# An encoder block with product-key experts on one core: lo parts on GpSimd, one more dense product ahead of the gate build, loads on another queue

## The chip, the cores and the metric

The program runs on one core of one Trainium2 chip. The metric is the time of one execution on the device in microseconds (us); lower is better. TensorE (PE) multiplies matrices, VectorE (DVE) and ScalarE (ACT) work element by element, GpSimd (POOL) does the gathers and a few small operations, and SyncE (SP), ScalarE and GpSimd issue DMAs.

## What is computed

One layer: adaLN modulation, an attention group and a gated MLP group side by side, an output projection, and then the PEER sub-layer, which takes most of the time. For each of 512 tokens and 8 heads it scores 2 x 128 keys, takes the best 16 of each half, the best 16 of the sums, and adds up 128 of 16384 one-neuron experts:

```python
def peer(h, w_q, keys, U, V):
    q = (ht @ w_q).reshape(T, PEER_HEADS, 2, PEER_HALF_DIM)
    s1 = jnp.einsum('thd,hkd->thk', q[:, :, 0], keys[:, 0])
    s2 = jnp.einsum('thd,hkd->thk', q[:, :, 1], keys[:, 1])
    v1, i1 = lax.top_k(s1, PEER_TOPK)
    v2, i2 = lax.top_k(s2, PEER_TOPK)
    cand = (v1[..., :, None] + v2[..., None, :]).reshape(T, PEER_HEADS, PEER_TOPK * PEER_TOPK)
    sc, ci = lax.top_k(cand, PEER_TOPK)
    idx = i1[ci // PEER_TOPK] * PEER_N_KEYS + i2[ci % PEER_TOPK]
    gates = jax.nn.softmax(sc, axis=-1)
    ...
        a = jnp.einsum('chkd,cd->chk', U[ids], xb)
        w = jax.nn.gelu(a, approximate=False) * g
        return jnp.einsum('chk,chkd->cd', w, V[ids])
```

All of it is float32. A float32 product is made of three TensorE products of a hi part (a rounded copy, made by ScalarE) and a lo part (what the rounding left, made by a subtraction): hi by hi, hi by lo, lo by hi (`mm3`, lines 84 to 88; `split_into`, lines 80 to 82).

## The kernel before

The experts are done in two ways. For the first 352 tokens they are dense: the 16384 experts are 128 tiles of 128, `a = gelu(U h2)` for every token and expert of tile e (a dense product, `a_mm`, 8 parts of 3 matmuls, tile `pa`), multiplied by a gate matrix that is zero for the experts not chosen, and then `w V` (tiles `out`). For the last 160 tokens, which are a block of 128 (the gathered block, names with g) and 32 more (names with x), the chosen rows of U and V are gathered by GpSimd and VectorE adds them up.

The stages of the second half, in order:

1. The score stage (the loop over `h` at line 729). `score(h)` makes two query products `q` (24 matmuls each, weights `wq`), copies them (`qT`), multiplies them with the keys (`sc`) and copies the scores to `s_sb` (dense tokens) and `s_gb`; the latter goes out to DRAM as `sgd`. Behind it `dense` products of the expert tiles from 2 on are placed, one for each head, and LATE = 8 more at the last head. Their operand comes from `a_load(e)`: a load of `u_t[e]`, and `split_into`, so a hi part (`u8h`) by ScalarE and a lo part (`u8l`) by VectorE; hi and lo have two buffers each, the loads three. Then VectorE takes the best 16 of each score row (`route_keys`, 5 operations each); after the fourth and the eighth head it does the candidates, picks and lookups of four heads, which end in `i1a` and `i2a`.
2. The gate build (lines 775 to 865), 44 steps for 8 tokens each: one-hot tiles `o` by VectorE and ScalarE, `gg` by TensorE, copies by ScalarE. Its order on TensorE, ScalarE and VectorE is written out by hand, and the dense products that are left up to tile 29 (`nu = AHEAD - ahead` of them) are laid in between, their loads and lo parts with them.
3. The expert loop (line 1051), 128 turns: a dense product 30 tiles ahead, the cast and lo part of V, the gates, and `out`. Between its turns a list of small jobs (`fill`) does the routing of the gathered block and its gathers. `gb_open` and `gb_scores` read that block's scores back from `sgd`, two heads in buffers (`sgb`).

Outside the hand-written parts the order of each engine's instructions is laid out when the program is built, by priorities in the order of the program and assumed costs. At run time each engine takes its own instructions in that order, and an instruction that waits for a semaphore holds those behind it on its engine, DMA issues included.

Of the kernel before, what the change touches and what calls it, by code (L numbers as in the profile page):

```python
# [25 lines left out]
PH = 8  # L26
# [9 lines left out]
NE = 128  # L36
AHEAD = 30
FIRST = 2
LATE = 8
TAIL = 4  # L40
END = 3
HG = 4
# [19 lines left out]
def tile_kernel(ctx: ExitStack, tc: tile.TileContext, a: dict, out: bass.AP):  # L62
    nc = tc.nc
# [16 lines left out]
    def split_into(hi, lo, src, eng=None):  # L80
        nc.scalar.copy(hi, src)
        last_lo[0] = (eng or nc.vector).tensor_sub(lo, src, hi.bitcast(F32))
# [27 lines left out]
    sgd = tc.dram_tile([P, 2 * PH, P], F32, name="sgd")  # L110
# [13 lines left out]
    with ExitStack() as fr:  # L124
# [141 lines left out]
        with ExitStack() as s1st:  # L266
# [43 lines left out]
            for kh in range(2):  # L310
                hi, lo = wl[kh]
# [158 lines left out]
        qkv_st.close()  # L470
        up = pool(ctx, "upool", side="right")

        def a_load(e):
            raw = up.tile([P, KD, P], F32, name=f"u{e}r", tag="ur", bufs=3)
            nc.sync.dma_start(raw, a["u_t"][e])
            hi = up.tile([P, KD, P], F32R, name=f"u{e}h", tag="uh", bufs=2)
            lo = up.tile([P, KD, P], F32R, name=f"u{e}l", tag="ul", bufs=2)
            split_into(hi, lo, raw)
            return hi, lo

        X = pool(right, "X2", side="right")
# [35 lines left out]
    def a_mm(e, p, hl, c):  # L517
        mm3(p[:, :TD], (hl[0][:, c, :], hl[1][:, c, :]), (h2T[0][:, c, :TD], h2T[1][:, c, :TD]),
            c == 0, c == KD - 1)

    def a_psum(e):
        return psa.tile([P, 512], F32, name=f"pa{e}", tag="pa", bufs=2)

    def a_gelu(e, p):
        t = ar.tile([P, TD], F32, name=f"a{e}", tag="a", bufs=AHEAD + 1)
        nc.scalar.activation(t, p[:, :TD], AF.Gelu)  # L526
        a_tiles[e] = t
# [17 lines left out]
    def route_tiles(pl, tag, nb, nh):  # L545
        r = {"nb": nb, "nh": nh, "pl": pl, "tag": tag}
        r["v12"] = pl.tile([P, nb, nh, 2, K], F32, name=f"v12{tag}", tag="v12", bufs=1)
        r["i12"] = pl.tile([P, nb, nh, 2, K], U32, name=f"i12{tag}", tag="i12", bufs=1)
        return r

    def route_keys(r, b, h, f, sv):
        tmp = r["pl"].tile([P, P], F32, name=f"tmp{r['tag']}{b}{h}{f}", tag="tmp", bufs=2)
        top16(r["v12"][:, b, h, f, :], r["i12"][:, b, h, f, :], sv, tmp)

    def route_cands(r):
        n = r["nb"] * r["nh"]
        v = r["v12"].rearrange("p b h f k -> p (b h) f k")
        cand = r["pl"].tile([P, n, NC], F32, name=f"cd{r['tag']}", tag="cand", bufs=1)
        for r0, nr, ncol, p0 in STAIR:
            sh = [P, n, nr, ncol]  # L560
            nc.vector.tensor_tensor(
                cand[:, :, p0:p0 + nr * ncol].rearrange("p b (i j) -> p b i j", j=ncol),
                v[:, :, 0, r0:r0 + nr].unsqueeze(3).to_broadcast(sh),
                v[:, :, 1, :ncol].unsqueeze(2).to_broadcast(sh), op=ALU.add)
        r["cand"] = cand
        r["ci"] = r["pl"].tile([P, n, K], U32, name=f"ci{r['tag']}", tag="ci", bufs=1)

    def route_pick(r, b, h, sc):
        i = b * r["nh"] + h
        cand2 = r["pl"].tile([P, NC], F32, name=f"ce{r['tag']}{i}", tag="cand2", bufs=2)  # L570
        top16(sc, r["ci"][:, i, :], r["cand"][:, i, :], cand2)

    def route_decode(r):
        pl, tag, ci = r["pl"], r["tag"], r["ci"]
        n = r["nb"] * r["nh"]
        rt_ = lambda m, dt=F32: pl.tile([P, n, K], dt, name=f"{m}{tag}", tag=m, bufs=1)
        t3, t2 = rt_("t3", U32), rt_("t2", U32)
        nc.vector.tensor_single_scalar(t3, ci, 3, op=ALU.logical_shift_right)
        nc.vector.tensor_single_scalar(t2, ci, 2, op=ALU.logical_shift_right)
        row, st, u = rt_("row"), rt_("rst"), rt_("ru")  # L580
        rcf = pl.tile([P, 2, n, K], BF16, name=f"rcf{tag}", tag="rcf", bufs=1)
        nc.vector.scalar_tensor_tensor(row, t3, 5.0, t2, op0=ALU.add, op1=ALU.max)
        nc.vector.scalar_tensor_tensor(row, row, 42.0, ci, op0=ALU.add, op1=ALU.max)
        nc.vector.tensor_scalar(row, row, -48.0, 0.0, op0=ALU.add, op1=ALU.max)
        nc.vector.tensor_copy(rcf[:, 0], row)
        nc.vector.tensor_scalar(st, row, 7.0, 8.0, op0=ALU.mult, op1=ALU.add)
        nc.vector.tensor_scalar(u, row, 3.0, 24.0, op0=ALU.mult, op1=ALU.add)
        nc.vector.scalar_tensor_tensor(st, row, 15.0, st, op0=ALU.mult, op1=ALU.min)
        nc.vector.scalar_tensor_tensor(st, u, 48.0, st, op0=ALU.min, op1=ALU.min)
        nc.vector.tensor_add(st, st, row)  # L590
        nc.vector.tensor_sub(rcf[:, 1], ci, st)
        r["rcf"] = rcf

    def route_tables(r):

        pl, tag = r["pl"], r["tag"]
        n = r["nb"] * r["nh"]
        i12f = pl.tile([P, n, 2, K], BF16, name=f"i12f{tag}", tag="i12f", bufs=1)
        nc.scalar.copy(i12f, r["i12"].rearrange("p b h f k -> p (b h) f k"))
        r["i12f"] = i12f  # L600
        r["rep"] = {}

    def route_rep(r, f):
        n = r["nb"] * r["nh"]
        t = r["pl"].tile([P, n, K, K], BF16, name=f"rep{r['tag']}{f}", tag="rep", bufs=1)
        nc.scalar.copy(t, r["i12f"][:, :, f, :].unsqueeze(3).to_broadcast([P, n, K, K]))
        r["rep"][f] = t
# [29 lines left out]
    with ExitStack() as qs:  # L637
# [45 lines left out]
        RD = pool(rd, "rdense", side="right")  # L683
        R = pool(qs, "route")
        keys = R.tile([P, 2 * PH, P], F32, name="keys_s")
        nc.gpsimd.dma_start(keys, a["keysT"])
        wq = {}

        def load_wq(i):
# [11 lines left out]
        def score(h):  # L701
            s_sb = R.tile([P, ND, 2, P], F32, name=f"s{h}", tag="s_sb", bufs=3)
            s_gb = R.tile([P, 2, P], F32, name=f"sg{h}", tag="s_gb", bufs=2)
            for f in range(2):
                i = 2 * h + f
                p = q_ps(f"q{i}")
                hi, lo = wq.pop(i)
                for j in range(KD):
                    mm3(p, (hi[:, j, :], lo[:, j, :]), (h2T[0][:, j, :], h2T[1][:, j, :]),
                        j == 0, j == KD - 1)  # L710
                if i + 2 < 2 * PH:
                    load_wq(i + 2)
                qT = W.tile([P, T], F32, name=f"qT{i}", tag="qT", bufs=3)
                nc.scalar.copy(qT, p)
                p = q_ps(f"sc{i}")
                for b in range(NB):
                    nc.tensor.matmul(p[:, b * P:(b + 1) * P], lhsT=qT[:, b * P:(b + 1) * P],
                                     rhs=keys[:, i, :], start=True, stop=True)
                nc.scalar.copy(s_sb[:, :, f, :], p[:, :TR].rearrange("p (b n) -> p b n", n=P))
                nc.scalar.copy(s_gb[:, f, :], p[:, TR:])  # L720
            nc.sync.dma_start(sgd[:, 2 * h:2 * h + 2, :], s_gb)
            scores[h] = s_sb

        i1a, i2a, sca, gts = [RD.tile([P, ND, PH, K], F32, name=n) for n in ("i1a", "i2a", "sca", "gts")]
        ahead = FIRST
        score(0)
        r = None
        nxt = a_load(ahead)
        for h in range(PH):
            if h + 1 < PH:  # L730
                score(h + 1)
            while ahead < FIRST + h + 1 + (LATE if h == PH - 1 else 0):
                hl, nxt = nxt, None
                p = a_psum(ahead)
                for c in range(KD):
                    a_mm(ahead, p, hl, c)
                nxt = a_load(ahead + 1)
                a_gelu(ahead, p)
                ahead += 1
            s_sb = scores.pop(h)  # L740
            hl = h % HG
            if hl == 0:
                r = route_tiles(R, f"d{h}", ND, HG)
            for b in range(ND):
                for f in range(2):
                    route_keys(r, b, hl, f, s_sb[:, b, f, :])
            if hl == HG - 1:
                hs = slice(h - HG + 1, h + 1)
                route_tables(r)
                route_rep(r, 0)  # L750
                route_cands(r)
                for b in range(ND):
                    for i in range(HG):
                        route_pick(r, b, i, sca[:, b, h - HG + 1 + i, :])
                route_decode(r)
                route_lookup(r, 0, i1a[:, :, hs, :])
                route_rep(r, 1)
                route_lookup(r, 1, i2a[:, :, hs, :])
# [16 lines left out]
    with ExitStack() as gs:  # L775
# [63 lines left out]
        for k in range(nu):  # L839
            e = ahead + k  # L840
            s0 = k * NG // nu
            st = {}
# [11 lines left out]
        ahead = AHEAD  # L854
# [18 lines left out]
    st = {}  # L873
# [9 lines left out]

    def gb_scores(h):
        st["sg"][h] = st["R"].tile([P, 2, P], F32, name=f"sgb{h}", tag="sg", bufs=2)
        nc.sync.dma_start(st["sg"][h], sgd[:, 2 * h:2 * h + 2, :])

    def gb_keys(h, f):
        if f == 0 and h + 1 < PH:
# [277 lines left out]
```

## Time and profile before

| what | value |
|---|---|
| median of 3 runs | 1520.97 us (1518.54 to 1521.08) |
| the profiled execution | 1520.59 us, of which the span of its instructions is 1518.8 us |
| TensorE busy | 1439.7 us (95%) |
| VectorE busy | 1287.3 us (85%) |
| ScalarE busy | 634.6 us (42%) |
| GpSimd busy | 489.4 us (32%) |
| DMA | 410.94 MB, mean 271 GB/s |

The busy time of TensorE counts matmuls from start to modelled end, so a full busy time is not yet TensorE at its peak. In the timelines each row is an instruction or several equal ones: start, length, engine, line, operation, what it writes and reads, shapes, and in brackets the idle time of that engine just before it and what ended it. The granted clock is the share of TensorE's full clock that it was given.

### The profile page before, as it was taken

How to read it: one execution, taken by the hardware profiler on the slowest of the kernel's cores; microseconds unless marked ns; L12 is line 12 of the kernel's file. 1: busy time of each engine (PE TensorE's matmuls, PEld its weight loads, DVE VectorE, ACT ScalarE, POOL GpSimd, SP SyncE). 2: the span in 40 equal slices, each digit the busy share in tenths (PEclk: the TensorE clock that was granted, in tenths of full speed). 3: DMA queues.
4: the chain of work that ended last, by engine and by line, in shares of the span. 5: the costliest groups of instructions: out<-in, count | busy, mean ns of one | idle time of the engine just before them, and what ended most of it. 6: DMA issues, size and time to landing. Idle time of an engine off the chain costs nothing.

```text
span 1518.8 us, 21628 instructions
## 1 busy us (share of the span) xinstructions
PE 1439.7 (95%) x7623; PEld 1235.6 (81%) x7623; DVE 1287.3 (85%) x2476; ACT 634.6 (42%) x1078; POOL 489.4 (32%) x400
## 2 busy tenths in 40 slices
PE   2899899999888999999999999999999999999997
PEld 1666677888788999888888888888888888888774
DVE  6947865569899997899999999998999999998776
ACT  2533433535257897333433333333333333333333
POOL 1212100000000000222354676666665555544420
PEclk9999999999998999999999999999999999999999
DMA  9626443332143779899799999999999999997863
GB/s 367 233 98 206 141 153 125 132 105 67 52 164 105 227 220 267 309 327 307 268 402 400 372 376 380 379 361 378 369 387 373 380 366 378 379 357 274 306 216 117
DMA packets 154332, 410.94 MB, mean 271 GB/s; under 512 B 13008, under 2 KB 58720, under 8 KB 154096
## 3 DMA queue, kind: packets, MB, share of 16 engines
q1 hardware_dynamic: 100720, 216.49, 40.1%
q0 software_dynamic: 51568, 187.17, 33.8%
q10 hardware_dynamic: 1936, 5.90, 1.1%
q8 instruction: 60, 0.98, 0.3%
q14 instruction: 48, 0.39, 0.1%
HBM read 381.24 MB, written 28.28 MB: 270 GB/s over the span
## 4 chain that ended last, share of the span: by engine, by line
PE 73%; DVE 13%; DMA 6%; ACT 4%; issue 3%; POOL 0%; SPq 0%; POOLq 0%; DVEq 0%; ACTq 0%
PE out L86 10%; PE out L88 10%; PE out L87 10%; PE pa L88 9%; PE pa L87 9%; PE pa L86 9%; DMA wada<-w_ada 2%; PE gg L822 2%; PE q L87 1%; PE q L88 1%; PE q L86 1%; ACT o L816 1%; PE yo L87 1%; PE yo L88 1%; PE yo L86 1%
## 5 line engine op out<-in xcount | busy, mean ns | idle before, releaser
L908 POOL DMA_INDIRECT gug<-peer_u,idx x128 | 200.3, 1565 | 104.6 <-DVE scrg L931 72.0
L908 POOL DMA_INDIRECT gvg<-peer_v,idx x128 | 162.0, 1266 | 159.6 <-DVE accg L945 141.0
L908 POOL DMA_INDIRECT gux<-peer_u,idxx x32 | 43.4, 1356 | 449.8 <-DMA u34r<-u_t 342.9
L945 DVE SCALAR_TENSOR_TENSOR accg<-gvg,wgg,accg 128x1024 f32<-128x1024 f32 x127 | 163.8, 1290 | 1.3
L931 DVE SCALAR_TENSOR_TENSOR scrg<-gug,h2gg 128x1024 bf16<-128x1024 f32 x128 | 156.2, 1221 | 1.3
L822 PE MATMUL gg<-o,o 128*128 128x128 f32 x704 | 88.4, 280 | 2.7 <-ACT o L816 1.6
L822 PEld LDWEIGHTS gg<-o,o 128*128 128x128 f32 x704 | 86.0, 196 | 4.7 <-ACT o L816 4.7
L1074 DVE TENSOR_TENSOR a<-a,g 128x352 f32<-128x352 f32 x128 | 64.9, 517 | 5.7 <-DMA g<-gd 3.4
L816 ACT ACTIVATE o<-o1b,gT 128x128 f32<-128x128 bf16 x176 | 58.2, 406 | 13.4 <-PE gg L822 6.8
L155 DVE SCALAR_TENSOR_TENSOR macc<-wada,csil,macc 128x1024 f32<-128x1024 f32 x40 | 51.3, 1282 | 10.8 <-DMA wada<-w_ada 10.5
L526 ACT ACTIVATE a<-pa 128x352 f32<-128x352 f32 x128 | 58.3, 456 | 1.5 <-PE pa L88 1.4
L805 DVE TENSOR_TENSOR o<-iota_s,gT 128x1024 f32<-128x1024 f32 x44 | 53.8, 1223 | 1.0 <-PE gg L822 0.9
L908 POOL DMA_INDIRECT gvx<-peer_v,idxx x32 | 40.2, 1256 | 33.4 <-DVE accx L945 23.6
L809 DVE TENSOR_SCALAR o<-iota_s,gT 128x128 f32<-128x128 f32 x176 | 49.1, 347 | 0.0
L831 ACT COPY st<-gg 128x512 f32<-128x512 f32 x88 | 46.3, 581 | 0.0
L931 DVE SCALAR_TENSOR_TENSOR scrx<-gux,h2gx 128x1024 bf16<-128x1024 f32 x32 | 39.0, 1218 | 3.3 <-DMA gux<-peer_u,idxx 3.3
L945 DVE SCALAR_TENSOR_TENSOR accx<-gvx,wgx,accx 128x1024 f32<-128x1024 f32 x31 | 40.0, 1291 | 0.3
L141 POOL DMA_DIRECT2D wada<-w_ada x32 | 17.2, 537 | 60.4 <-DVE macc L155 24.4
L165 PE MATMUL mcol<-ident_s,macc 128*128 128x128 f32 x32 | 7.4, 389 | 27.4 <-DVE macc L152 23.2
L165 PEld LDWEIGHTS mcol<-ident_s,macc 128*128 128x128 f32 x32 | 5.5, 200 | 29.0 <-DVE macc L152 18.1
L430 ACT ACTIVATE pe<-s,mx 128x512 f32<-128x512 f32 x16 | 11.0, 690 | 28.9 <-DVE mx L428 21.6
L120 POOL TENSOR_TENSOR n_r<-n_ms,nhalf 128x1 f32<-128x1 f32 (+1 forms) x5 | 3.6, 717 | 54.7 <-DVE n_ms L118 54.7
(2817 smaller groups left out, 4971.7 us busy)
## 6 DMA issues: line engine op xcount, KB each, us to landing
gd<-st SPq DMA_DIRECT2D x11, 1984.0 KB
g<-gd SPq DMA_DIRECT2D x31, 704.0 KB
wada<-w_ada POOLq DMA_DIRECT2D x32, 512.0 KB
wada<-w_ada SPq DMA_DIRECT2D x16, 512.0 KB
x<-x SPq DMA_DIRECT2D x4, 512.0 KB
x<-x ACTq DMA_DIRECT2D x4, 512.0 KB
x2d<-x ACTq DMA_DIRECT2D x4, 512.0 KB
gug<-peer_u,idx POOLq DMA_INDIRECT x128
```

Source lines behind the costliest of these rows:

```text
L86: nc.tensor.matmul(o, lhsT=lh, rhs=rh, start=first, stop=False)
L87: nc.tensor.matmul(o, lhsT=lh, rhs=rl, start=False, stop=False)
L88: nc.tensor.matmul(o, lhsT=ll, rhs=rh, start=False, stop=last)
L155: nc.vector.scalar_tensor_tensor(acc, w, csil[:, c:c + 1], acc, op0=ALU.mult, op1=ALU.add)
L526: nc.scalar.activation(t, p[:, :TD], AF.Gelu)
L805: nc.vector.tensor_tensor(o2s[n], iota.unsqueeze(1).to_broadcast([P, UT, P]), tT[:, 1, t0:t0 + UT].unsqueeze(2).to_broadcast([P, UT, P]), ...
L816: nc.scalar.activation(o1s[n][:, i, :], e[:, :, i], AF.Copy, scale=tT[:, 2, t0 + i:t0 + i + 1])
L822: nc.tensor.matmul(pgs[n][i // 4][:, i % 4 * P:(i % 4 + 1) * P], lhsT=o2[:, i, :], rhs=o1[:, i, :], start=True, stop=True)
L908: nc.gpsimd.indirect_dma_start(out=g, out_offset=None, in_=src, in_offset=bass.IndirectOffsetOnAxis(ap=ix[:, s:s + 1], axis=0))
L931: nc.vector.scalar_tensor_tensor(scr, g, 1.0, gs_[k]["h2g"], op0=ALU.mult, op1=ALU.mult, accum_out=actg[:, n:n + 1])
L945: nc.vector.scalar_tensor_tensor(accg, g, wg[:, s:s + 1], accg, op0=ALU.mult, op1=ALU.add)
L1074: nc.vector.tensor_tensor(wv3, wv3, gt[:, :, e % GE, :], op=ALU.mult)
```

## The change

Three things. `a_load` takes an engine for the subtraction, and the score loop passes GpSimd for tiles 2 to 9, placed on GpSimd's queue behind the load of the keys. LATE goes from 8 to 9, so that tile 18's dense product stands in the score loop and the gate build has 11 in place of 12. And the loads of the gathered block's scores go on ScalarE's queue in place of SyncE's.

```diff
-LATE = 8
+LATE = 9
...
-        def a_load(e):
+        def a_load(e, eng=None):
             raw = up.tile([P, KD, P], F32, name=f"u{e}r", tag="ur", bufs=3)
             nc.sync.dma_start(raw, a["u_t"][e])
             hi = up.tile([P, KD, P], F32R, name=f"u{e}h", tag="uh", bufs=2)
             lo = up.tile([P, KD, P], F32R, name=f"u{e}l", tag="ul", bufs=2)
-            split_into(hi, lo, raw)
+            with ExitStack() as order:
+                if eng is not None:
+                    order.enter_context(tc.issue_after(keyed.ins))
+                split_into(hi, lo, raw, eng)
             return hi, lo
...
-        nc.gpsimd.dma_start(keys, a["keysT"])
+        keyed = nc.gpsimd.dma_start(keys, a["keysT"])
...
-        nxt = a_load(ahead)
+        nxt = a_load(ahead, nc.gpsimd)
...
-                nxt = a_load(ahead + 1)
+                nxt = a_load(ahead + 1, nc.gpsimd if ahead + 1 < FIRST + PH else None)
...
-        nc.sync.dma_start(st["sg"][h], sgd[:, 2 * h:2 * h + 2, :])
+        nc.scalar.dma_start(st["sg"][h], sgd[:, 2 * h:2 * h + 2, :])
```

## Rows read from the trace of the kernel before

**Rows 1.** Windows: stretch, length; PE, PEld, DVE, ACT, POOL busy; PEclk, DMA share, GB/s.

```profile
290.00:350.00 60.00, 60.00 (x302) 50.32 (x301) 39.03 (x192) 17.77 (x32) 0.00 (x0) 1.00 0.31 96
350.00:400.00 50.00, 45.76 (x222) 38.36 (x221) 48.90 (x238) 21.26 (x31) 0.00 (x0) 0.93 0.18 59
400.00:460.00 60.00, 50.99 (x293) 47.02 (x292) 53.39 (x231) 26.77 (x34) 0.00 (x0) 0.95 0.36 119
620.00:700.00 80.00, 75.82 (x393) 65.84 (x392) 76.37 (x216) 29.50 (x43) 24.10 (x17) 1.00 0.91 328
800.00:900.00 100.00, 100.00 (x526) 88.40 (x526) 91.81 (x118) 35.67 (x50) 60.90 (x42) 1.00 1.00 383
```

**Rows 2.** Timeline of TensorE, score stage: q12, u8l's wait, q15.

```profile
376.99 0.48 PE L86 MATMUL q<-h2T,wq12h 128*128 128x512 f32 x1
...
387.06 0.66 PE L88 MATMUL pa<-h2T,u8l 128*128 128x352 f32 x1 [3.93 <-DVE u8l L82]
...
406.24 0.48 PE L86 MATMUL q<-h2T,wq15h 128*128 128x512 f32 x1
```

**Rows 3.** Timeline of ScalarE, score stage: casts of u8, wq11, wq12.

```profile
355.42 1.08 ACT L81 CAST u8h<-u8r 128x1024 fp32r<-128x1024 f32 x1
358.18 1.05 ACT L81 CAST wq11h<-wq11r 128x1024 fp32r<-128x1024 f32 x1 [1.68 <-PE q L87]
...
366.31 1.05 ACT L81 CAST wq12h<-wq12r 128x1024 fp32r<-128x1024 f32 x1 [4.70 <-PE q L87]
```

**Rows 4.** Timeline of VectorE, score stage: u8l, and its longest idle time.

```profile
385.78 1.23 DVE L82 TENSOR_TENSOR u8l<-u8r,u8h 128x1024 fp32r<-128x1024 f32 x1
...
414.21 1.22 DVE L82 TENSOR_TENSOR u10l<-u10r,u10h 128x1024 fp32r<-128x1024 f32 x1 [5.00 <-ACT u10h L81]
```

**Rows 5.** Timeline of VectorE and TensorE, start of the score stage: u2.

```profile
270.46 1.22 DVE L82 TENSOR_TENSOR u2l<-u2r,u2h 128x1024 fp32r<-128x1024 f32 x1
...
272.69 0.32 PE L88 MATMUL pa<-h2T,u2l 128*128 128x352 f32 x1
...
272.85 0.33 PE L86 MATMUL pa<-h2T,u2h 128*128 128x352 f32 x1
```

**Rows 6.** GpSimd's groups by shape: count | busy us, mean ns | idle us.

```profile
L120 POOL TENSOR_TENSOR rq_r<-rq_ms,nhalf 128x4 f32<-128x4 f32 x1 | 1.0, 1037 | 5.8 <-DVE rq_ms L118 5.8
...
L100 POOL MEMSET ones<- 128x128 f32 x1 | 0.2, 229 | 0.0
...
L102 POOL MEMSET nhalf<- 128x8 f32 x1 | 0.1, 129 | 0.0
```

**Rows 7.** Timeline of TensorE ahead of the gate build.

```profile
458.93 0.47 PE L782 MATMUL gt<-ident_s,i2a 128*128 128x128 f32 x1 [5.82 <-DVE i2a L623]
```

**Rows 8.** Timeline of VectorE in the gate build: one operation of three steps.

```profile
501.04 1.22 DVE L805 TENSOR_TENSOR o<-iota_s,gT 128x1024 f32<-128x1024 f32 x1
...
505.38 1.22 DVE L805 TENSOR_TENSOR o<-iota_s,gT 128x1024 f32<-128x1024 f32 x1
...
507.87 1.22 DVE L805 TENSOR_TENSOR o<-iota_s,gT 128x1024 f32<-128x1024 f32 x1
```

**Rows 9.** Timeline of SyncE's DMA issues, start of the expert loop.

```profile
594.88 4.30 SPq L475 DMA_DIRECT2D u34r<-u_t  x1
...
599.74 0.90 SPq L886 DMA_DIRECT2D sgb<-sgd  x2
...
617.76 0.32 SPq L886 DMA_DIRECT2D sgb<-sgd  x1
```

**Rows 10.** Timeline of VectorE, start of the expert loop.

```profile
605.97 0.49 DVE L539 MAX8 v12g<-sgb 128x8 f32<-128x128 f32 x2 [3.49 <-DMA sgb<-sgd]
...
615.49 0.29 DVE L539 MAX8 v12g<-sgb 128x8 f32<-128x128 f32 x1 [3.88 <-DMA sgb<-sgd]
```

**Rows 11.** Timeline of ScalarE, start of the expert loop.

```profile
622.67 1.05 ACT L1070 CAST v4h<-v4r 128x1024 fp32r<-128x1024 f32 x1 [9.44 <-DMA v4r<-peer_v]
```

**Rows 12.** Timeline of TensorE, start of the expert loop.

```profile
622.10 0.50 PE L88 MATMUL out<-v3h,w3l 128*128 128x512 f32 x1 [1.72 <-DVE w3l L82]
```

## The prediction

> **What bounds the kernel now.** I read the page first, then the windows by stage, then the timelines of the places where TensorE stands idle. On the page TensorE is the busiest engine by far, so a change pays where it takes idle time or a slow clock from TensorE. The windows show where that is [rows 1]. From 800 us on TensorE is busy 100.00 of 100 us, and from 290 to 350 us 60.00 of 60. Idle time lies between 350 and 460 us (4.24 and 9.01 us, at a granted clock of 0.93 and 0.95) and between 620 and 700 us (4.18 us). The loop behind 700 us is full of TensorE's work, so what is won ahead of it should come out at the end almost whole.
>
> **The score stage.** Between the scores TensorE works in a fixed order: a query product `q`, some matmuls of a dense product `pa`, the score matmuls `sc`. From the start of q12 to that of q15, three such steps, it takes 406.24 - 376.99 = 29.25 us [rows 2]. A regular step is 8.13 us: ScalarE casts the query weights once a step, wq11h at 358.18 and wq12h at 366.31 us [rows 3]. In the first of the three steps the order has `pa` matmuls on u8's lo part ahead of the scores, and TensorE stands 3.93 us for it [rows 2]. The hi part had been there since 355.42 + 1.08 = 356.50 us [rows 3]; the lo part ran on VectorE only at 385.78 us [rows 4], behind the routing of the first four heads. The slow clock of this window comes with that stall.
>
> **Removing that wait.** With u2 to u9 on GpSimd, u8l can be made right behind u8h, some 25 us before it is wanted. Three regular steps are 24.39 us, so the last scores come 29.25 - 24.39 = **4.9 us** earlier. What is late next? VectorE, which must be done with the earlier heads by then. Ahead of the last scores it idles 5.00 us [rows 4], and it loses two lo parts of 1.23 us (u8, u9); so at least 5.00 + 2.46 - 4.9 = 2.6 us of idle time are left, and the scores still end last. The other six lo parts (u2 to u7) fall where VectorE is busy 39.03 of 60 us and TensorE all 60 [rows 1]: they win nothing. From 414 us on VectorE is the chain, until i2a, the last index that the gate build waits for; all of this moves up by 4.9 us. Bounds: 0, if another wait takes the place of u8l's; 7.7 us, if all that TensorE loses from 350 to 400 us comes back (4.24 us idle and 0.07 of 50 us by the clock [rows 1]).
>
> **What a lo part costs on GpSimd.** The trace has no such subtraction on that engine. On VectorE it takes 1.22 us [rows 5], the lower bound. On GpSimd a memset of 128 columns takes 0.229 us and one of 8 columns 0.129 us [rows 6], so 0.0008 us a column and 0.9 us for 1024; two reads and a write at that rate give 2.7 us, which I take. The far end is a `pow` row, 1.037 us for 4 columns [rows 6], which would be over 260 us for 1024. I hold that for the price of `pow` and give it 1 in 100. A dense product lasts about two steps, 16 us, in this stage, and two lo buffers stand ready, so anything under 16 us hides behind the queries. The exception is u2, the first: its lo part began at 270.46 and TensorE used it at 272.69 us [rows 5]; at 2.7 us it is ready at 273.1, **0.4 us** late (0 to 1.5). GpSimd's queue has nothing else in this stage; the load of the keys is kept ahead of the lo parts by the order that the change adds.
>
> A rule speaks against the move. The Trainium skill, "GPSIMD Engine Reference", 3.1, has a two-input add take 1.96 times as long as on VectorE, and the Trainium skill, "SBUF — State Buffer", Who interferes with whom, says that a VectorE instruction with two SBUF inputs and a GpSimd instruction that reads SBUF shut each other out for their whole length. By these, as an estimate, a lo part takes 2.4 us and can hold VectorE as long; no run here shows it yet. For u8 and u9 that would be 4.8 us where 2.6 us are left, and the sum would be 2.2 us worse.
>
> **Nine dense products.** One `pa` product (u18) moves from the gate build to the stretch ahead of it, and with it u19's load, cast and lo part. TensorE's 24 matmuls, 3.84 us at 0.16 us from start to start [rows 5], fit into the 5.82 us for which it waits for i2a [rows 7]. VectorE, which sets that end, gets one lo part more: +1.2 us. In the gate build a VectorE step takes 507.87 - 505.38 = 2.49 us, and one with a lo part in it 505.38 - 501.04 = 4.34 us [rows 8]; one less there is worth 1.85 us. Net **-0.6 us**. Bounds: +1.2 us, if nothing comes back in the build; -2.6 us, if TensorE is its true limit and the whole 3.84 us come back.
>
> **Scores on ScalarE's queue.** The loads of the gathered block's scores, `sgb`, stand in SyncE's order behind loads that wait. The first goes out at 599.74 us, behind u34r's issue of 4.30 us [rows 9]; VectorE stands 3.49 us for it until 605.97, and 3.88 us for the third until 615.49 us [rows 10]. SyncE in its turn stands until 617.76 us at the fifth [rows 9], and v4r behind it goes out only then; ScalarE idles 9.44 us for v4r [rows 11]. TensorE loses 1.72 us waiting for w3l [rows 12], which VectorE makes behind all this. On ScalarE the first load need not wait for u34r and can go some 5 us earlier, and v4r no longer stands behind the fifth. I take the wait for w3l as gone, **-1.7 us**. The eight issues cost ScalarE 0.32 to 0.45 us each, as on SyncE [rows 9], in a stretch where it is busy 29.50 of 80 us [rows 1]. From the third on a load waits until VectorE has read the scores two loads before, and behind it on ScalarE stand the casts of u, v and w. Bounds: -4.2 us, all of TensorE's idle time from 620 to 700 us, and +2 us, if casts are held.
>
> **The sum.** -4.9 + 0.4 - 0.6 - 1.7 = -6.8 us. The profiled execution took 1520.59 us, 1.8 of it outside the span, and lies 0.4 us under the median of 1520.97. 1520.6 - 6.8 = **1513.8 us**.
>
> **The rivals.**
> *The wait moves.* The order of every engine is laid out anew at the build, from assumed costs. The 3.93 us come from one misjudged place, and another may arise: VectorE held in the routing of the first four heads, or TensorE placed ahead of a lo part on GpSimd. For it: VectorE is busy 48.90 of 50 us there [rows 1]. Against it: the 25 us of lead. Then 1.3 of the 4.9 us are left and half of the queue's share: -1.3 + 0.4 - 0.6 - 0.9 = -2.4, 1518.2 us, up to 1520.
> *More comes out.* Half-way from the sum to all the good bounds (-7.7 - 2.6 - 4.2 = -14.5): -10.7, 1509.9 us.
> *ScalarE is held (slower).* A load of `sgb` that stands ahead of casts holds them until VectorE has caught up. One hold of 9.44 us [rows 11] came with 1.72 us lost on TensorE [rows 12]. Six loads wait for a buffer; if each is laid so far ahead of its release, that is 6 x 1.7 = 10 us in place of the 1.7 won: 1520.6 - 5.1 + 10 = 1525.5 us. It decides from holds over about 9 us. Against it: the casts have gaps there, and every load wants a buffer that VectorE frees in its own order.
> *Nothing.* If the last scores don't set the end of the routing, the small terms are left, 1519 us.
>
> **How the numbers follow.** Forecast (its own range 1511 to 1517) 0.57; the wait moves 0.16; more comes out 0.11; ScalarE held 0.13; nothing 0.03. About 0.2%, 3.0 us, is what a measurement of this kernel can tell from no change. Faster by more, under 1517.9: forecast and more comes out, 0.68. Slower, over 1524.0: 0.13. Within: 0.19. The range goes from 1508 to 1522 us: it takes in the moved wait and the bounds that are not at their ends together, and leaves out most of the slower case.
>
> **What would show it.** Right: u8l and u9l on GpSimd soon behind their casts, 2 to 3 us each; no TensorE wait over 1 us among the queries; q12 to q15 in some 24.4 us; i2a 3.7 us earlier (TensorE goes on at 455 in place of 458.93); the first `sgb` at VectorE by 601 us; no 1.7 us wait for w3l. Wrong: VectorE's two-input operations longer beside GpSimd; a new wait among the queries; ScalarE idle with a load of `sgb` at its head while TensorE waits for a cast; a gain that is there by 460 us and gone by 700.

## The result and the profile after

| what | before | after |
|---|---|---|
| median | 1521.03 us (1518.54 to 1521.65) | 1510.43 us (1509.14 to 1511.65) |
| ratio, 95% interval | | 0.9937 [0.9922, 0.9953] |
| profiled execution (span) | 1520.59 us (1518.8) | 1509.24 us (1507.5) |

The kernel is faster by 0.6%; the forecast of 1513.8 us is 3.4 us above the median, and its sign and range hold. The two profiled executions differ by 11.3 us, where the working had 6.8. The windows by stage, which answer to [rows 1], show TensorE's idle time from 350 to 400 and from 620 to 700 us gone, and 3.75 of 9.01 us of that between 400 and 460 us (columns as in [rows 1]):

```profile
350.00:400.00 50.00, 50.00 (x258) 42.37 (x257) 49.93 (x243) 23.04 (x33) 9.04 (x3) 1.00 0.20 62
400.00:460.00 60.00, 54.74 (x321) 51.09 (x319) 55.35 (x227) 30.14 (x43) 0.00 (x0) 0.97 0.42 135
620.00:700.00 80.00, 80.00 (x424) 70.94 (x423) 79.78 (x228) 30.73 (x46) 22.33 (x16) 1.00 0.91 328
```

The timeline of TensorE holds what answers to [rows 2, 7]: q12, q15, i2a. No row in between has a wait for u8l, and the three steps take 403.43 - 378.79 = 24.64 us in place of 29.25.

```profile
378.79 0.39 PE L86 MATMUL q<-h2T,wq12h 128*128 128x512 f32 x1
...
403.43 0.48 PE L86 MATMUL q<-h2T,wq15h 128*128 128x512 f32 x1
...
457.20 0.47 PE L785 MATMUL gt<-ident_s,i2a 128*128 128x128 f32 x1 [2.37 <-DVE i2a L626]
```

But q12 itself starts 1.80 us later than before, though the front of the kernel ran 0.53 us ahead in this profile. Here is the start of the score stage on TensorE, which answers to [rows 5], with GpSimd's first lo part:

```profile
269.99 2.35 POOL L82 TENSOR_TENSOR u2l<-u2r,u2h 128x1024 fp32r<-128x1024 f32 x1 [10.40 <-ACT u2h L81]
...
274.26 0.33 PE L674 MATMUL h2gp<-ident_s,tg 128*128 128x128 f32 x1 [0.70 <-ACT tg L193]
275.67 0.64 PE L86 MATMUL q<-h2T,wq0h 128*128 128x512 f32 x1 [1.08 <-ACT h2T L81]
276.93 0.79 PE L87 MATMUL q<-h2T,wq0h 128*128 128x512 f32 x1 [0.61 <-DVE h2T L82]
...
285.32 0.32 PE L88 MATMUL pa<-h2T,u2l 128*128 128x352 f32 x1
```

u2l is ready at 272.34 us, yet its first matmul stands at 285.32, behind q0. Before, u2's product filled the time up to q0 [rows 5]; now the build's order has put 22 of its 24 matmuls behind q0, TensorE stands idle three times for the activations that q0 needs (2.39 us), and q0 then runs at a slow clock. The queries themselves are hardly late by that: counted from the first transposes of the stage, q1 to q9 start only 0.5 us later than before. What is lost at first is dense work. In the timelines 58 dense matmuls stand ahead of q1 where 97 stood, and part of the missing ones comes back ahead of later queries: the step from q9 to q10 holds 14 of them in place of 9, that from q11 to q12 15 in place of 7, and these two steps are 0.88 and 1.03 us longer. Windows of the dense products alone (PE, PEld, ACT busy; PEclk, DMA share, GB/s), up to q1 and for the two steps, first before, then after:

```profile
260.00:287.50 27.50, 17.74 (x97) 15.55 (x97) 1.28 (x3) 1.00 0.60 210
352.55:360.67 8.12, 1.60 (x9) 1.50 (x9) 0.00 (x0) 1.00 0.20 67
368.81:376.98 8.17, 1.28 (x7) 1.18 (x7) 0.47 (x1) 1.00 0.18 62
...
260.00:287.46 27.46, 10.79 (x58) 9.20 (x58) 0.82 (x2) 0.88 0.37 132
352.49:361.50 9.01, 2.48 (x14) 2.28 (x14) 0.00 (x0) 1.00 0.19 60
369.57:378.78 9.21, 2.64 (x15) 2.45 (x15) 0.00 (x0) 1.00 0.17 57
```

Where the 11.3 us lie, from stage to stage of the two timelines (each difference against the stage before it):

| stretch | worked out | trace |
|---|---|---|
| front, up to the first transposes of the score stage | 0 | -0.53 |
| from there to q12 (u2's lo part) | +0.4 | +2.33 |
| q12 to q15 (u8's wait) | -4.9 | -4.61 |
| q15 to i2a (u19's lo part) | +1.2 | +1.08 |
| gate build | -1.85 | -3.82 |
| expert loop up to v20 | -1.7 | -5.19 |
| the rest | 0 | -0.6 |

### The profile page after: what moved, and what is told of

It reads as the page before. It is cut to its first block, busy times and chain, and to the rows that moved or that the text cites. A ratio compares the mean times of both kernels' runs of the same rounds, so it can differ in the third digit from the quotient of the medians.

```text
span 1507.5 us, 21637 instructions
## 1 busy us (share of the span) xinstructions
PE 1440.5 (96%) x7623; PEld 1235.2 (82%) x7623; DVE 1280.5 (85%) x2468; ACT 634.4 (42%) x1078; POOL 509.5 (34%) x408
## 4 chain that ended last, share of the span: by engine, by line
PE 78%; DVE 9%; ACT 4%; DMA 4%; issue 4%; POOL 1%; SPq 0%; POOLq 0%; ACTq 0%; DVEq 0%
PE out L86 11%; PE out L87 11%; PE out L88 11%; PE pa L88 9%; PE pa L87 9%; PE pa L86 9%; DMA wada<-w_ada 2%; PE q L87 2%; PE q L86 2%; PE q L88 2%; ACT o L819 2%; PE gg L825 1%; DVE o L812 1%; PE sc L720 1%; PE yo L86 1%
## 5 line engine op out<-in xcount | busy, mean ns | idle before, releaser
L542 DVE MAX8 v12d<-s 128x8 f32<-128x128 f32 x48 | 12.8, 285 | 11.4 <-ACT s L722 11.4
```

## The experiments

All ratios are to runs of the kernel before made beside them on the same chip, and a time won or lost against it is by the ratio. An interval is some 2 us to each side, so two kernels are told apart from about 3 us on; finer readings are from the traces. The front varies by itself: the first transposes of the score stage start between 255.56 and 259.39 us in the profiles of kernels that do the same up to there, so times below are counted from them ("from the front").

### Each part alone

The lo parts alone (LATE back at 8, `sgb` back on SyncE):

```diff
-LATE = 9
+LATE = 8
...
-        nc.scalar.dma_start(st["sg"][h], sgd[:, 2 * h:2 * h + 2, :])
+        nc.sync.dma_start(st["sg"][h], sgd[:, 2 * h:2 * h + 2, :])
```

> The lo parts of tiles 2 to 9 on GpSimd alone; LATE stays 8 and the scores stay on SyncE's queue. Theory A, the three parts add up: in the changed kernel q15 starts 2.8 us earlier than before, and without the tenth tile's work VectorE's tail moves by as much, so 2.8 us faster (1518.2 against 1521.0), with no TensorE wait for u8l and about 2.4 us of idle time at the start of the score stage. Theory B, the lo parts only make room for the ninth dense product: under 1 us faster, about 1520.5, because the matmuls of u2 to u8 that were put off in the score stage come back ahead of the gate build.

Measured: 1516.21 us, ratio 0.9974 [0.9965, 0.9982], 4 us less, more than either theory had.

Nine dense products alone, on the kernel before:

```diff
-LATE = 8
+LATE = 9
```

> LATE = 9 alone; all lo parts on VectorE, scores on SyncE's queue. Theory A: the gate build is 3.8 us shorter, as in the changed kernel (128.6 to 124.8 us from its first to its last matmul), and VectorE's tail one lo part longer (1.2 us), so 2.6 us faster, 1518.4. Theory B, LATE and the lo parts carry one gain between them: under 1.5 us faster, 1519.5 or more, because VectorE, which sets the tail, also has u8 and u9 to do. By the prediction's own term it would be 0.6 us.

Measured: 1512.38 us, 0.9949 [0.9933, 0.9965], 7.8 us less, and the wait of 3.94 us for u8l is still in it. At most a third of the gain was expected, 2.6 us. By its trace the gate build gives 3.79 us and the loop up to v20 5.46 us, while i2a comes 1.0 us later from the front.

ScalarE's queue alone, on the kernel before:

```diff
-        nc.sync.dma_start(st["sg"][h], sgd[:, 2 * h:2 * h + 2, :])
+        nc.scalar.dma_start(st["sg"][h], sgd[:, 2 * h:2 * h + 2, :])
```

> The loads of the gathered block's scores on ScalarE's queue alone. Theory A: all that the changed kernel wins behind the gate build, 5.6 us (1515.4), with no TensorE wait over 0.4 us between 600 and 720 us and the first scores at VectorE 5 us or more earlier. Theory B: part of those 5.6 us is owed to the earlier gate build, and the queue alone gives what the prediction had, 1.7 us (1519.3).

Measured: 1515.28 us, 0.9971 [0.9960, 0.9982], 4.4 us less, between the two theories. The three ratios multiplied give 0.9894, the whole change 0.9937: the parts overlap.

### Two parts at a time

The changed kernel without the queue:

```diff
-        nc.scalar.dma_start(st["sg"][h], sgd[:, 2 * h:2 * h + 2, :])
+        nc.sync.dma_start(st["sg"][h], sgd[:, 2 * h:2 * h + 2, :])
```

> The changed kernel with the gathered block's scores read on SyncE's queue as before: two of the three parts. Theory A (the queue pays for the same TensorE waits in the expert loop, for w3l, w4l and v12l, that are gone with nine dense products alone, so the parts overlap): within 1 us of the changed kernel's 1510.4 us; no TensorE wait over 0.5 us between 600 and 720 us. Theory B (the prediction's: the queue is worth 1.7 us or more by itself in the changed kernel): 1.7 to 4.5 us slower than the changed kernel, with a TensorE wait for w3l in the trace.

Measured: 1511.43 us, 0.9952 [0.9940, 0.9965]. The time can't decide between the two, the trace can: the wait for w3l is there with 1.68 us, those for v12l and u44l are not. In its loop up to v20, 2.3 us less is gained than in the changed kernel. So each theory is half right.

Nine products and the queue, without the lo parts on GpSimd:

```diff
-LATE = 8
+LATE = 9
...
-        nc.sync.dma_start(st["sg"][h], sgd[:, 2 * h:2 * h + 2, :])
+        nc.scalar.dma_start(st["sg"][h], sgd[:, 2 * h:2 * h + 2, :])
```

> Nine dense products and ScalarE's queue, with all lo parts on VectorE. Theory A (overlap in the expert loop): as nine dense products alone, 7 to 9 us under the kernel before, so 1512 to 1514 us; u8's wait of 3.9 us still there. Theory B (additive): 7.8 + 4.4 = 12 us under, some 1508 us. Its distance to the changed kernel is what the lo parts bring there: by the wait of u8's lo part, 3 us or more were it not for u2's.

Measured: 1513.15 us, 0.9958 [0.9946, 0.9971], as nine products alone: the queue adds nothing there that shows.

### Which waits the loop's gain is made of

Two waits on VectorE stand behind TensorE's idle time in the loop. The first is that for the gathered block's scores, with the rows of [rows 10, 12]. Here it is in the changed kernel without the queue, on VectorE and TensorE:

```profile
600.33 0.49 DVE L542 MAX8 v12g<-sgb 128x8 f32<-128x128 f32 x2 [3.46 <-DMA h2gx<-h2gd]
609.85 0.30 DVE L542 MAX8 v12g<-sgb 128x8 f32<-128x128 f32 x1 [3.87 <-DMA sgb<-sgd]
...
616.46 0.50 PE L88 MATMUL out<-v3h,w3l 128*128 128x512 f32 x1 [1.68 <-DVE w3l L82]
```

| kernel | VectorE's two waits at `sgb` | TensorE's wait for w3l | difference |
|---|---|---|---|
| before [rows 10, 12] | 3.49 + 3.88 = 7.37 | 1.72 | 5.65 |
| lo parts and nine products | 3.46 + 3.87 = 7.33 | 1.68 | 5.65 |
| lo parts alone | 3.60 + 3.68 = 7.28 | 1.63 | 5.65 |
| u2's lo part alone | 3.46 + 3.55 = 7.01 | 1.36 | 5.65 |
| u8's and u9's lo parts alone | 3.77 + 3.09 = 6.86 | 1.20 | 5.66 |
| nine products alone | 2.14 + 1.63 = 3.77 | none | |
| after | 2.53 | none | |

(The two kernels with single lo parts come further down.) In each kernel TensorE's wait is what VectorE stands at these two reads beyond 5.65 us. In three of them the profile puts the first wait down to h2gx, a load that SyncE issues right behind the first scores; the instruction itself reads `sgb`. The trace shows too why nine products alone were rid of it with the loads on SyncE: there the first `sgb` came to VectorE 604.66 - 599.57 = 5.1 us after its issue, in place of 605.97 - 599.74 = 6.2 us [rows 9, 10]. Why it landed sooner is open.

The second is further on, in the kernel before: VectorE stands for a load of the gate matrix, and TensorE behind it for v12l.

```profile
695.04 0.53 DVE L1074 TENSOR_TENSOR a<-a,g 128x352 f32<-128x352 f32 x1 [3.15 <-DMA g<-gd]
...
696.76 0.50 PE L87 MATMUL out<-v12l,w12h 128*128 128x512 f32 x1 [1.95 <-DVE v12l L1071]
```

It stands in each of the four kernels with LATE at 8 and the scores on SyncE (1.95, 1.05, 1.10, 2.00 us on TensorE), and in none with nine products or with ScalarE's queue. With the small ones for w4l and u44l (0.52 and 0.39 us in before) it makes 2.9 us that either part takes away (but for 0.15 us at w4l in the kernel with lo parts and nine products), and that can be won only once. By what path each of the two edits takes this wait away is open.

### The lo parts taken apart

The changed kernel with u2's lo part back on VectorE:

```diff
-        nxt = a_load(ahead, nc.gpsimd)
+        nxt = a_load(ahead)
```

> The changed kernel with u2's lo part, the first one, back on VectorE; the rest as in the changed kernel (1510.4 us). Theory A: the 2.4 us of idle time and the slow clock at the start of the score stage, with u2's matmuls put off, come from this one lo part; they go, q12 to q15 start about 2 us earlier, and as TensorE has next to no idle time from there to the gate build, the kernel gets 2 us faster than the changed one, 1508.4. Theory B: what is lost there is made up by TensorE ahead of the gate build anyway: within 0.5 us of the changed kernel.

Measured: 1505.91 us, 0.9907 [0.9891, 0.9923], 4.5 us under the changed kernel: more than twice what was expected. The idle time at the start of the stage is gone.

The changed kernel with only u8's and u9's lo parts on GpSimd:

```diff
-        nxt = a_load(ahead, nc.gpsimd)
+        nxt = a_load(ahead)
...
-                nxt = a_load(ahead + 1, nc.gpsimd if ahead + 1 < FIRST + PH else None)
+                nxt = a_load(ahead + 1, nc.gpsimd if FIRST + PH - 2 <= ahead + 1 < FIRST + PH else None)
```

> The changed kernel with only the lo parts of u8 and u9 on GpSimd, those of u2 to u7 on VectorE as before. Theory A (the whole gain of the lo parts in the score stage is u8's wait; u2's costs some 4.5 us by the order that its late lo part brings to TensorE, u3 to u7 nothing): as the kernel with u2 alone put back, 1505.9 us within 1 us. Theory B (u3 to u7 on GpSimd free VectorE for the scores' copies as well): 1 to 3 us slower than that.

Measured: 1504.79 us, 0.9911 [0.9897, 0.9926]. u3 to u7 bring nothing to the whole on GpSimd. With them there (the run before this one) the queries are earlier, q15 at 141.29 us from the front against 143.63 here, but this is lost again behind q15: VectorE stands 1.73 us for the cast of u18, and i2a comes at 196.99 against 196.51 us.

The same two lo parts, alone on the kernel before (that edit, with LATE at 8 and `sgb` on SyncE):

> The kernel before with the lo parts of u8 and u9 alone on GpSimd: the prediction's first term by itself. Theory A (that term was right, and what spoiled it in the whole change was u2's lo part): q12 to q15 in 24.5 us, i2a and the whole kernel 4.5 to 6 us earlier, ratio 0.9962 to 0.997. Theory B (the wait moves into the tail or VectorE is shut out beside GpSimd): under 3 us.

Measured: 1513.24 us, 0.9952 [0.9934, 0.9970], 7.3 us less; from the front q15 is 5.6 and i2a 6.4 us earlier. On TensorE q12 and q15 now start 23.73 us apart:

```profile
377.64 0.48 PE L86 MATMUL q<-h2T,wq12h 128*128 128x512 f32 x1
...
401.37 0.48 PE L86 MATMUL q<-h2T,wq15h 128*128 128x512 f32 x1
```

So the first term of the prediction was no smaller than it said.

u2's lo part alone on GpSimd, on the kernel before:

```diff
-                nxt = a_load(ahead + 1, nc.gpsimd if ahead + 1 < FIRST + PH else None)
+                nxt = a_load(ahead + 1)
...
-LATE = 9
+LATE = 8
...
-        nc.scalar.dma_start(st["sg"][h], sgd[:, 2 * h:2 * h + 2, :])
+        nc.sync.dma_start(st["sg"][h], sgd[:, 2 * h:2 * h + 2, :])
```

> The kernel before with u2's lo part alone on GpSimd, the prediction's second term by itself: 0.4 us there. Theory A (the build puts off u2's matmuls and TensorE stands ahead of the first query): q12 1.5 to 3 us later and the whole kernel 1 to 4.5 us slower. Theory B (0.4 us): no difference that can be measured.

Measured: 1516.01 us, 0.9971 [0.9960, 0.9983], 4.4 us *less*. Both theories are wrong about the total. q12 is late, as theory A has it (2.6 us from the front). But the three steps behind it take 403.88 - 379.24 = 24.64 us: the wait for u8l is gone although VectorE still makes u8l at 387.4 us, behind the routing. u2's put-off matmuls come back ahead of the later queries, all dense products stand a place later, and u8l's first matmul is at 402.4 us. The timelines of VectorE and of TensorE:

```profile
387.42 1.22 DVE L82 TENSOR_TENSOR u8l<-u8r,u8h 128x1024 fp32r<-128x1024 f32 x1
...
402.39 0.32 PE L88 MATMUL pa<-h2T,u8l 128*128 128x352 f32 x1
```

With the lo parts alone (0.9974) it is the same. In the changed kernel, then, u2's late product had already moved the dense products out of the way of u8's wait, at the price of a later q12; the other seven lo parts on GpSimd bring nothing that shows. Without u2, u8 and u9 alone bring the whole of it.

The changed kernel with u2's product tied ahead of q0 on TensorE:

```diff
-        score(0)
-        r = None
         nxt = a_load(ahead, nc.gpsimd)
+        p2 = a_psum(ahead)
+        for c in range(KD):
+            last2 = a_mm(ahead, p2, nxt, c)
+        with tc.issue_after(last2.ins):
+            score(0)
+        r = None
...
-                p = a_psum(ahead)
-                for c in range(KD):
+                p = p2 if ahead == FIRST else a_psum(ahead)
+                for c in range(KD if ahead > FIRST else 0):
```

> The changed kernel, u2's lo part on GpSimd, with u2's whole dense product tied ahead of the first query's matmuls on TensorE. Theory A (the cost is that of the order in which the build laid TensorE's work, not of GpSimd's 2.4 us): the idle time and the slow clock ahead of the first queries are gone but for 0.5 to 1 us, 3 to 5 us under the changed kernel, so 1505.5 to 1507.5 us. Theory B (the late lo part itself costs it): within 1 us of the changed kernel's 1510.4.

Measured: 1513.07 us, 0.9956 [0.9940, 0.9972], 2.6 us over the changed kernel by the medians: neither the gain of theory A nor, within its 1 us, theory B. Timeline of TensorE and GpSimd at the start of the stage, and of VectorE ahead of i2a:

```profile
269.69 2.35 POOL L82 TENSOR_TENSOR u2l<-u2r,u2h 128x1024 fp32r<-128x1024 f32 x1 [10.66 <-ACT u2h L81]
...
277.31 0.66 PE L86 MATMUL pa<-h2T,u3h 128*128 128x352 f32 x1 [3.02 <-ACT u3h L81]
277.76 0.49 PE L87 MATMUL pa<-h2T,u3h 128*128 128x352 f32 x1
278.06 0.49 PE L88 MATMUL pa<-h2T,u2l 128*128 128x352 f32 x1
...
452.78 1.23 DVE L82 TENSOR_TENSOR u18l<-u18r,u18h 128x1024 fp32r<-128x1024 f32 x1 [2.93 <-ACT u18h L81]
```

u2l is ready at 272.04 and used at 278.06 us; what TensorE waits for, 3.02 us, is u3's hi part, whose matmuls the build now laid ahead. So in neither kernel does TensorE wait for GpSimd's 2.35 us; the order around the lo part is what differs. The total of this run doesn't prove that by itself, because the edit changed the order elsewhere too: from the front q15 is only 1.1 us later than in the changed kernel (148.04 against 146.92), but i2a 4.3 us (204.95 against 200.69), as VectorE stands 2.93 us for the cast of u18, a wait that the changed kernel hasn't got. Which of the build's assumed costs makes it lay u2 out so isn't settled; an order that keeps u2 on GpSimd and loses nothing was not found.

### A tenth product, and the queue in the best version

u2's lo part on VectorE and ten products ahead:

```diff
-LATE = 9
+LATE = 10
...
-        nxt = a_load(ahead, nc.gpsimd)
+        nxt = a_load(ahead)
```

> The changed kernel with u2's lo part back on VectorE and ten dense products ahead of the gate build. Theory A (VectorE sets the last scores, so u20's lo part puts i2a off by 1.2 us, and in the gate build one product fewer gives back up to 3.8 us where VectorE is the limit): 1 to 3 us under the kernel with u2 alone put back, so 1503 to 1505 us. Theory B (the gate build's gain came from the even spacing of 11 products over 44 steps, which 10 don't have): the same or slower than 1505.9 us.

Measured: 1505.45 us, 0.9918 [0.9905, 0.9931]: the same as with nine. The windows from the first to the last `gg` of the gate build show why; the kernels are before (12 products in the build), nine products alone (11), and this one (10):

```profile
462.04:590.66 128.62, 127.45 (x985) 125.85 (x985) 123.10 (x274) 114.98 (x294) 0.00 (x0) 0.98 0.70 202
```

```profile
465.39:590.22 124.83, 123.24 (x957) 121.26 (x958) 121.72 (x273) 112.72 (x291) 0.00 (x0) 0.98 0.70 203
```

```profile
458.18:581.82 123.64, 118.68 (x940) 116.47 (x940) 120.38 (x272) 112.02 (x290) 0.00 (x0) 1.00 0.69 199
```

With 12 products TensorE is busy 127.45 of 128.62 us and is the limit, so the first product taken out gives 3.79 us, nearly all of its 3.84. With 10, TensorE idles 4.96 us, VectorE is busy 120.38 of 123.64 us, and the second one gives 1.19 us. Ahead of the build it costs more than one lo part: from the front the first `gg` comes at 201.90 in place of 199.85 us, 2.05 us later. With nine products TensorE had only 1.39 us of waiting for i2a left to fill, and with ten it is still at u19's matmuls when VectorE is done with i2a (454.23 us; the last of them starts at 455.07). So nothing is left. Theory B had the time right, but its reason, even spacing, isn't needed.

u8 and u9 on GpSimd with nine products, the scores on SyncE:

```diff
-        nc.scalar.dma_start(st["sg"][h], sgd[:, 2 * h:2 * h + 2, :])
+        nc.sync.dma_start(st["sg"][h], sgd[:, 2 * h:2 * h + 2, :])
```

> The best kernel so far (only u8's and u9's lo parts on GpSimd, nine dense products, ScalarE's queue: 1504.8 us) with the scores' loads back on SyncE's queue. Theory A (nine dense products alone empty the pool of TensorE waits in the expert loop, as in the run with them alone): within 1 us of it, no TensorE wait over 0.5 us between 600 and 710 us. Theory B (the wait for w3l stays, as in the changed kernel without the queue): 1.7 to 3 us slower, 1506.5 to 1508 us, with a wait of 1.2 to 1.7 us for w3l.

Measured: 1507.35 us, 0.9921 [0.9903, 0.9939], beside 0.9911 with the queue, and between what the two theories had. VectorE's two waits at `sgb` are 3.21 + 3.22 = 6.43 us, less 5.65 gives 0.78, and the wait for w3l is 0.78 us:

```profile
610.94 0.50 PE L88 MATMUL out<-v3h,w3l 128*128 128x512 f32 x1 [0.78 <-DVE w3l L82]
```

Up to v20 its loop gains 1.6 us less than with the queue: what the queue is worth once nine products have taken the rest.

**The best version** is the one with only u8 and u9 on GpSimd, nine products and ScalarE's queue, 1504.79 us; u2 alone put back can't be told from it, though TensorE there stands 1.49 us for u33l in the loop. Both lie 4 to 5.6 us under the changed kernel, by ratios and by medians; their intervals just overlap that of the changed kernel, 0.9926 and 0.9923 against 0.9922.

## Why the prediction was right, step by step

**u8's wait: right.** -4.61 us against -4.9 between q12 and q15, and -5.5 us with u8 and u9 alone. The last scores still ended last: VectorE idles 3.53 us for them, where 2.6 were worked out from 5.00 [rows 4], and 0.58 us with u8 and u9 alone, where u10's lo part is made ahead of that wait. The row of 5.00 us was read a little wrongly. It ends with the cast of u10, which ScalarE made right ahead of copying the last scores, and VectorE came to the scores at 415.35 us, behind u10l. In the changed kernel the cast stands behind the scores. ScalarE in the kernel before, then VectorE in the changed one:

```profile
412.90 1.05 ACT L81 CAST u10h<-u10r 128x1024 fp32r<-128x1024 f32 x1 [0.16 <-PE pa L87]
413.99 0.48 ACT L719 COPY s<-sc 128x384 f32<-128x384 f32 x1
...
411.69 0.49 DVE L542 MAX8 v12d<-s 128x8 f32<-128x128 f32 x2 [3.53 <-ACT s L722]
```

**u2's lo part: the step that failed.** The lo part took 2.35 us, against 2.7 estimated, so its price was right; the cost of +0.4 us was not, because it was worked out in the old order of TensorE. The build laid the order anew, and from the front to q12 it cost 2.33 us. The prediction named a new order at the build as a rival, but with TensorE waiting for a lo part; here TensorE never waits for u2l, its work with it was put off. Put back, u2 is worth 4.5 us by the medians; and since the same order also takes u8's wait away, the changed kernel was not the sum of the two terms.

**Nine dense products: right sign, mis-sized.** The tail cost +1.08 us against +1.2 (u18's and u19's lo parts both lie ahead of i2a). In the gate build 3.82 us came back where 1.85 was taken. The step mis-sized is that VectorE's step length was taken for the limit there; TensorE is, by the window above, and the bound worked out from its 24 matmuls (3.84 us) was the value. With 1.08 it makes -2.7 us in place of -0.6.

**The queue: right for w3l, and short by the rest.** The first scores were at VectorE at 596.46 us (by 601 was asked), v4r was issued at 602.56 in place of 618.18 us, and the wait for w3l is gone: 1.72 us against 1.7. But the loop's other waits, 2.9 us, went too: with w3l's they make 4.58 of the 5.19 us, more than the bound of -4.2 us, which took in 620 to 700 us alone. And they are no more the queue's than the ninth product's, as each alone shows. The rival in which ScalarE is held did not come: the longest hold was 4.08 us, in the timeline of ScalarE, and TensorE shows no wait between 600 and 720 us.

```profile
600.80 3.98 ACTq L889 DMA_DIRECT2D sgb<-sgd  x2
604.82 1.05 ACT L1073 CAST v3h<-v3r 128x1024 fp32r<-128x1024 f32 x1 [4.08 <-DMA sgb<-sgd]
```

**The total** came within 3.4 us because a loss that was too small (2 us) stood against two gains that were too small (2.1 and 3.5 us). To that extent it is luck.

## What to carry to other kernels

Where a program's order is laid out at the build, an edit that gives an instruction to another engine can change the order of all who use its result: price the edit by its smallest version (here the two lo parts that were waited for) and leave the others alone. Before pricing a product moved out of a stage, divide both engines' busy time by that stage's length; here the one at 99% gave its own time back, and the next edit of the kind met the other engine. Two edits that aim at the same idle time are not added: list the waits of the stretch, and note which edit takes which.

## What the runs showed of the hardware

**VectorE and GpSimd held each other up.** In the changed kernel u8l took 4.08 us on GpSimd beside two-input operations of VectorE, and one of these took 2.28 us, until just after u8l's end at 384.09; before, that operation took 0.34 us. Timelines of the changed kernel, and last of the kernel before:

```profile
380.01 4.08 POOL L82 TENSOR_TENSOR u8l<-u8r,u8h 128x1024 fp32r<-128x1024 f32 x1 [14.73 <-ACT u8h L81]
...
382.02 2.28 DVE L624 TENSOR_TENSOR ohd<-ohd 128x384 bf16<-128x384 bf16 x1
...
381.50 0.34 DVE L621 TENSOR_TENSOR ohd<-ohd 128x384 bf16<-128x384 bf16 x1
```

With u8 and u9 alone, u9l meets a longer run of such operations and takes 5.52 us, beside 2.40 for u8l; with u2 alone put back, u8l takes 7.35 us. These are the rows that the rule of the Trainium skill, "SBUF — State Buffer", Who interferes with whom, speaks of, and they agree with it. The 2.2 us that the prediction worked out from it for the sum did not come: VectorE still idles for the last scores (3.53 us, and 0.58 us with u8 and u9 alone). The Trainium skill's 1.96 times ("GPSIMD Engine Reference", 3.1) agrees as well: 2.35 to 2.42 us undisturbed, against 1.22 on VectorE [rows 5].

**After short pauses TensorE ran slow for longer than they had lasted.** After the three pauses of 2.39 us between 273.56 and 276.93 us the granted clock was 0.50, the lower level of 1.2 GHz, from 277 to 282.5 us, and the matmuls of q0 started 0.43 us apart; afterwards, 0.23. Windows of the changed kernel, and of the kernel before:

```profile
277.00:282.50 5.50, 5.50 (x13) 4.34 (x14) 0.00 (x0) 0.56 (x1) 2.37 (x1) 0.50 0.22 90
...
277.30:282.80 5.50, 5.50 (x24) 4.48 (x25) 2.45 (x2) 2.02 (x4) 0.00 (x0) 1.00 0.67 208
```

13 matmuls started in 5.5 us, where before, from 277.3 to 282.8 us, it was 24 at a clock of 1.00. At 0.23 us each 13 take 3.0 us, so 2.5 us were lost to the clock, as much as to the pauses. This is no fixed price: in the changed kernel without the queue the same three pauses (2.54 us) stand there, and q0's matmuls are back at 0.23 us apart from 281.0 us on, 3.8 us after the last pause.
